# Layer 0's mixer of a two-layer decoder trunk: projections in seven block products, and the order of the output gate and the decays

## The chip, the cores and the metric

One core of a Trainium2 chip runs the whole program: two decoder layers on a sequence of 512 tokens of 1024 features. The metric is the device time of one execution in microseconds (us); the number given is a median over runs.

## The reference

Each layer is a half-step SwiGLU feed-forward, a mixer, and another half-step feed-forward. The change is inside the mixer of layer 0, the "hybrid" mixer (condensed):

```python
def hybrid_mixer(h, w_in, ...):                       # h: 512 x 1024, already normalised
    z, xbc, dt_raw, qm, km, vm, om, ig, fg = split_cols(h @ w_in, HY_SPLITS)
    xbc = jax.nn.silu(causal_dwconv(xbc, conv_w, conv_b))
    xs, bm, cm = split_cols(xbc, ...)                 # 1024, 256, 256 wide
    dt = jax.nn.softplus(dt_raw + dt_bias)
    y = ssd_chunked(xs, dt, A, bm, cm, 128) + xs * d_skip   # 16 heads, scan over chunks
    y = rms_norm(y * silu(z), ssd_norm)               # in 2 groups of 512 features
    hm = mlstm_chunked(qm, km, vm, ig + igate_bias, fg + fgate_bias, 128)   # 4 heads
    hm = rms_norm(hm, mlstm_norm) * sigmoid(om)       # per head of 256 features
    return concatenate([y, hm]) @ w_out               # 2048 -> 1024
```

The parts of `h @ w_in` are Z (1024 columns), xBC (1536), the gates (24), queries and keys (512 each), values (1024) and the output gate `om` (1024). All is float32. A float32 product is done on TensorE as three products of rounded parts: with x = xh + xl and w = wh + wl it takes xh·wh + xh·wl + xl·wh.

## The kernel before

**Engines and forms.** TensorE (PE) multiplies. A block of weights is loaded by SyncE (SP) into one of four `raw` buffers (128 x 1024 floats, 512 KB) and brought into a `form` buffer of high and low parts: `split` (L236 to L242) copies the high part on ScalarE (ACT, L239) and subtracts it on VectorE (DVE, L242). The feed-forward has a second way, a "summed" form: ACT writes the negated rounded copy into the low part's place (L529), GpSimd (POOL) issues a DMA that adds the raw block to it (L530), and ACT writes the high part (L531); DVE takes no part. `form` (L257) has the same way, but only for the mixer of layer 1. `mm3` (L277 to L282) issues the three matmuls of a product; PSUM collects the sum.

**Feed-forward: seven block products.** Both sides of a product are cut into 2x2 blocks, and seven products of sums and differences of blocks give the four blocks of the result, in place of eight (`seven`, L621). It needs seven block combinations of the activations (`xf`), four subtractions of weight blocks, and additions out of PSUM. The order on each engine is worked out by a planner (`Plan`).

**Mixer of layer 0.** Here the engines' order is the program's order, and generators are interleaved by `weave(main, filler, ratio)` (L53): after each step of `main`, `ratio` steps of `filler` are issued. Every engine works through its own list in that order, so an instruction that waits holds up what stands behind it on its engine. `hybrid` (L947) does, one after the other:

1. xBC by six pieces of 256 columns (`conv`), woven with the gates. All projections use `xgn`, the activations times the norm's gain as high and low parts; the row factor of the norm (`rrow`, or `rcol` for token-major output) is applied when PSUM is read.
2. `ssd`, the scan: 16 steps (4 chunks of 128 tokens, 4 quarters of 4 heads). A quarter's `decays` loads rows of cumulated decay by DMA, subtracts (DVE), masks (POOL `affine_select`), takes the exponential (ACT) and multiplies (DVE); `outputs` multiplies it with the values on TensorE. The decays are issued one quarter ahead of the outputs. Filler of the weave, at 1.35 to 1: queries, keys (`gemm_feat`, tile pqk), values, output gate (`gemm_tok`, tile ptok), in matmuls that stream 512 columns.
3. `mlstm`, 4 chunks; each multiplies its numerator (`pn`) into the output gate's tile `og`, and at the chunk's end scales it by the norm's factor. Then `og` is transposed (pht) into `hh`, `hl`. Filler, at 0.8 to 1: `gate`, that is Z (tile pz, 512 columns), SiLU, product with the scan's output and its norm by groups.
4. `project`: `[y, hm] @ w_out` (tile po), added to the residual, in weight pieces of rows 0 to 4, 8 to 16 and 4 to 8 (times 128).

Tiles come from pools by name and tag; a tile whose buffers are all taken waits for the release of the oldest. PSUM has 4 banks for tag mm, and pairs of banks (`ps_two`, tags pA and pB) that the feed-forward uses.

Of the kernel before, what the change touches and what calls it, by code (L numbers as in the profile page):

```python
# [44 lines left out]
NMIX = dict(mix0=10, mix1=15)  # L45
# [168 lines left out]
class Trunk:  # L214
# [21 lines left out]
    def split(self, hi, lo, src, eng="act"):  # L236
        nc = self.nc
        if eng == "act":
            nc.scalar.activation(hi, src, AF.Copy)  # L239
        else:  # L240
            nc.vector.tensor_copy(hi, src)
        nc.vector.tensor_tensor(lo, src, hi.bitcast(F32), op=ALU.subtract)  # L242
# [14 lines left out]
    def form(self, raw):  # L257
# [181 lines left out]

    def spread(self, cols, n, name):  # L440
# [10 lines left out]
    def rows_from(self, src, name):  # L451

        rows = self.tmp.tile([P, 4, P], F32, name=name, tag="rows", bufs=4)
        self.nc.sync.dma_start(rows, src.rearrange("n p -> (n p)").partition_broadcast(P).rearrange("q (n p) -> q n p", p=P))
        return rows
# [316 lines left out]
    def prep_later(self, which, k, last, squares=True, half=None):  # L772
# [5 lines left out]
        if k == 0 and not half:  # L778
            self.which = which
            self.xgn = [[Lazy(lambda: self.part.tile([P, 4, T], F32R, name="xgn", tag="xg")) for _ in range(2)] for _ in range(2)]  # L780
            squares4 = Lazy(lambda: self.tmp.tile([P, 4, T], F32, name="ssq", tag="ssq", bufs=1))
# [165 lines left out]
    def hybrid(self, nxt):  # L947
# [6 lines left out]
        weave(  # L954
            self.gates(w, ((0, DT0, 16), (16, F0, 4), (20, I0, 4)), g),
            chain(*(self.conv(w, X0, cp, xs, bc) for cp in (4, 5, 0, 1, 2, 3))),
            1.0,
        )

        q, k = self.slot("q"), self.slot("k")  # L960
        v = self.tmp.tile([P, 2, 2, 4, 257], F32, name="v", tag="v", bufs=1)
        v = [v[:, i] for i in range(2)]
        og = []

        def projections():
            for t, c0, sc in ((q, Q0, 128 ** -0.5), (k, K0, 1.0)):
                for cp in range(2):
                    W = self.wload(w[:, c0 + cp * 256 : c0 + cp * 256 + 256])
                    W = list(W)
                    for m in range(2):  # L970
                        ps = self.mmps("pqk")
                        self.gemm_feat(ps, W, m)
                        self.mark = nc.vector.scalar_tensor_tensor(
                            t[:, 2 * cp + m], ps, sc, self.rrow, op0=ALU.mult, op1=ALU.mult
                        )
                        yield
            for t in v:
                with self.tc.issue_after(self.mark.ins):
                    nc.vector.memset(t[:, :, :, 256:257], 1.0)
            for h in (0, 2):  # L980
                yield from self.gemm_tok(w, V0 + h * 256, 512, lambda b, ps, h=h: nc.scalar.activation(
                    v[b // 2][:, b % 2, h : h + 2, 0:256], ps.rearrange("p (h n) -> p h n", h=2), AF.Copy,
                    scale=self.rcol[:, b : b + 1]))
            og.extend(self.slot("og", F32, (2, 4, 256)) for _ in range(2))
            for h in (0, 2):
                yield from self.gemm_tok(w, O0 + h * 256, 512, lambda b, ps, h=h: nc.scalar.activation(
                    og[b // 2][:, b % 2, h : h + 2], ps.rearrange("p (h n) -> p h n", h=2), AF.Sigmoid,
                    scale=self.rcol[:, b : b + 1]))

        weave(self.ssd(xs, bc, g), projections(), 1.35)  # L990

        hid = [None] * 16

        def mlstm():
            yield from self.mlstm(q, k, v, og, g)
            hh, hl = self.feat("hh", KC, F32R), self.feat("hl", KC, F32R)
            for c in range(KC):
                pt = self.aux("pht", (T,))
                for b in range(NB):
                    nc.tensor.transpose(  # L1000
                        pt[:, b * P : (b + 1) * P], og[b // 2][:, b % 2, c // 2, (c % 2) * P : (c % 2 + 1) * P],
                        self.ident,
                    )
                self.split_gain(hh[c], hl[c], pt, self.par[:, 116 + c : 117 + c])
                hid[KC + c] = (hh[c], hl[c])
                if c % 2:
                    yield

        weave(mlstm(), self.gate(w, Z0, xs, hid), 0.8)
        self.project(a["hy_w_out"][0], hid, 1.0, nxt, ((0, 4), (8, 16), (4, 8)), 2)  # L1010

# [22 lines left out]
    def gate(self, w, Z0, xs, hid):  # L1034

        nc = self.nc
        for grp in range(2):
            for cp in range(2):
                c0 = Z0 + grp * 512 + cp * 256
                W = list(self.wload(w[:, c0 : c0 + 256]))  # L1040
                for m in range(2):
                    c = 4 * grp + 2 * cp + m
                    ps = self.mmps("pz")
                    self.gemm_feat(ps, W, m)
                    t1 = self.tmp.tile([P, T], F32, name="t1", tag="t1")
                    nc.vector.tensor_tensor(t1, ps, self.rrow, op=ALU.mult)
                    nc.scalar.activation(t1, t1, AF.Silu)
                    nc.vector.tensor_tensor(xs[c], xs[c], t1, op=ALU.mult)
                    if c % 4 == 0:
                        ssq = self.tmp.tile([P, T], F32, name="ssq", tag="ssq", bufs=1)  # L1050
                        nc.scalar.activation(ssq, xs[c], AF.Square)
                    else:
                        sq = self.tmp.tile([P, T], F32, name="sq", tag="t2")
                        nc.scalar.activation(sq, xs[c], AF.Square)
                        nc.vector.tensor_tensor(ssq, ssq, sq, op=ALU.add)
                    yield
# [3 lines left out]
            nc.scalar.activation(r, self.rows_of(rc).rearrange("p a b -> p (a b)"), AF.Copy)  # L1060
            yh, yl = self.slot("yh", F32R), self.slot("yl", F32R)
            for j in range(4):
                c = 4 * grp + j
                nc.vector.tensor_tensor(xs[c], xs[c], r, op=ALU.mult)
# [3 lines left out]
    def gemm_tok(self, w, c0, n, evac):  # L1068

        ps = [self.mmps("ptok", (512,)) for _ in range(NB)]  # L1070
        for k0 in range(0, KC, 2):
            W = self.form(self.raw(w[k0 * P : (k0 + 2) * P, c0 : c0 + n].rearrange("(k p) n -> p k n", p=P), 2, n))
            for b in range(NB):
                tok = slice(b * P, (b + 1) * P)
                for j in range(2):
                    k = k0 + j
                    self.mm3(
                        ps[b][:, 0:n],
# [815 lines left out]
```

## Time and profile before

| | |
|---|---|
| time, median of 3 runs | 2016.77 us (2015.88 to 2018.02) |
| the profiled execution's own time | 2019.29 us |
| its span, first to last instruction | 2017.6 us |
| mean granted TensorE clock | 0.992 |
| layer 0's mixer in it, about | 353 to 757 us |
| DVE forms of layer 0's mixer (L242, 128x1024) | 60 in the whole run, 1240 ns each |
| accumulating DMAs (form<-raw, POOL) | 136, of which none in this mixer |

A row of instruction groups reads: line, engine, operation, output<-input with shape, xcount | busy us, mean ns of one | idle time of the engine just before them, with what ended it. A row of windows reads: stretch, its length, busy us (count) of PE, PE's weight load, DVE, ACT, POOL, granted clock (1.00 is full), DMA share, GB/s. A row of the timeline reads: start, duration, engine, line, operation, tiles.

### The profile page before, as it was taken

What the parts mean: (1) busy time and instruction counts of PE and PEld (TensorE: products, weight loads), DVE (VectorE), ACT (ScalarE), POOL (GpSimd) and SP (SyncE); (2) the same over time, 40 slices, a digit from 0 to 9 for tenths busy, and PEclk for the clock granted to TensorE, in tenths of its full rate; (3) what the DMA queues carried; (4) which work ended last, traced back from release to release, by engine and by line L of the source; (5) the groups of instructions that cost most, each with busy time, mean ns of one, the idle gap of its engine ahead of it and who ended that gap; (6) DMA issues with size and microseconds to landing.
All of it is one profiled execution on the core that took longest, in us unless ns stands there. A gap on an engine that the chain in (4) does not pass through costs nothing.

```text
span 2017.6 us, 34412 instructions
## 1 busy us (share of the span) xinstructions
PE 1984.4 (98%) x13892; PEld 1800.6 (89%) x13892; DVE 1581.4 (78%) x2340; ACT 1170.2 (58%) x1716; POOL 270.1 (13%) x335
## 2 busy tenths in 40 slices
PE   8999999999999999999999999999999999999998
PEld 6999999787788888999998899999965678999998
DVE  6898878886547648988888898978679847988886
ACT  6666657442345434666565575756667644757565
POOL 1000101321101011010002010101215321101010
PEclk9999999999999999999999999999899999999999
DMA  7556566433331232666565356656754202656564
GB/s 210 136 148 167 150 164 148 125 107 115 103 96 63 82 97 63 168 157 162 155 152 149 94 148 167 161 153 160 191 116 105 53 16 69 157 158 165 150 168 115
DMA packets 214439, 265.49 MB, mean 132 GB/s; under 512 B 14140, under 2 KB 187400, under 8 KB 214280
## 3 DMA queue, kind: packets, MB, share of 16 engines
q1 hardware_dynamic: 193632, 190.87, 30.5%
q0 software_dynamic: 20448, 72.36, 19.2%
q8 instruction: 109, 1.79, 0.4%
q14 instruction: 50, 0.41, 0.1%
q10 hardware_dynamic: 200, 0.06, 0.0%
HBM read 188.77 MB, written 2.14 MB: 95 GB/s over the span
## 4 chain that ended last, share of the span: by engine, by line
PE 86%; DVE 5%; DMA 4%; issue 2%; ACT 1%; POOL 1%; SPq 0%; ACTq 0%; POOLq 0%; DVEq 0%
PE pA L281 9%; PE pA L280 9%; PE pA L282 9%; PE pD L280 5%; PE pD L281 5%; PE pD L282 5%; PE pB L280 2%; PE pB L281 2%; PE pB L282 2%; DMA form<-raw 2%; PE po L280 2%; PE po L282 2%; PE po L281 2%; PE ptok L280 2%; PE pu L282 2%
## 5 line engine op out<-in xcount | busy, mean ns | idle before, releaser
L502 DVE TENSOR_TENSOR form<-raw,form 128x1024 fp32r<-128x1024 f32 (+1 forms) x327 | 388.0, 1191 | 113.2 <-ACT form L500 112.3
L500 ACT ACTIVATE form<-raw 128x1024 fp32r<-128x1024 f32 (+1 forms) x327 | 334.6, 1027 | 177.3 <-DVE raw L495 120.6
L280 PE MATMUL pA<-xf,form 128*128 128x256 f32 x1152 | 322.1, 280 | 0.0
L281 PE MATMUL pA<-xf,form 128*128 128x256 f32 x1152 | 321.8, 279 | 0.0
L282 PE MATMUL pA<-xf,form 128*128 128x256 f32 x1152 | 321.4, 279 | 0.0
L495 DVE TENSOR_TENSOR raw<-raw 128x1024 f32<-128x1024 f32 (+2 forms) x241 | 283.6, 1180 | 17.4 <-DMA raw<-in_ffn_w_down 8.6
L530 POOL DMA_DIRECT2D form<-raw x136 | 116.9, 860 | 1202.7 <-ACT form L529 1142.4
L529 ACT ACTIVATE form<-raw 128x1024 fp32r<-128x1024 f32 (+1 forms) x136 | 140.1, 1031 | 140.3 <-PE pD L282 77.4
L280 PEld LDWEIGHTS pA<-xf,form 128*128 128x128 f32 x1152 | 216.4, 188 | 0.2
L282 PEld LDWEIGHTS pA<-xf,form 128*128 128x128 f32 x1152 | 216.1, 188 | 0.0
L281 PEld LDWEIGHTS pA<-xf,form 128*128 128x128 f32 x1152 | 215.8, 187 | 0.2
L281 PE MATMUL pA<-hid,form 128*128 128x256 f32 x704 | 198.6, 282 | 2.8 <-DVE hid L502 2.8
L280 PE MATMUL pA<-hid,form 128*128 128x256 f32 x704 | 198.8, 282 | 0.5 <-ACT hid L500 0.4
L282 PE MATMUL pA<-hid,form 128*128 128x256 f32 x704 | 197.4, 280 | 0.0
L280 PE MATMUL pD<-xf,form 128*128 128x256 f32 x576 | 161.2, 280 | 0.0
L281 PE MATMUL pD<-xf,form 128*128 128x256 f32 x576 | 161.2, 280 | 0.0
L282 PE MATMUL pD<-xf,form 128*128 128x256 f32 x576 | 161.0, 280 | 0.0
L495 DVE TENSOR_TENSOR ft<-ft 128x256 f32<-128x256 f32 (+2 forms) x288 | 146.1, 539 | 4.6 <-ACT ft L748 1.2
L531 ACT ACTIVATE form<-raw 128x1024 fp32r<-128x1024 f32 (+1 forms) x136 | 138.6, 1021 | 0.0
L281 PEld LDWEIGHTS pA<-hid,form 128*128 128x128 f32 x704 | 132.3, 188 | 4.7 <-DVE hid L502 4.6
L280 PEld LDWEIGHTS pA<-hid,form 128*128 128x128 f32 x704 | 132.6, 188 | 1.3 <-ACT hid L500 0.6
L282 PEld LDWEIGHTS pA<-hid,form 128*128 128x128 f32 x704 | 132.3, 188 | 0.0
(447 smaller groups left out, 5191.5 us busy)
## 6 DMA issues: line engine op xcount, KB each, us to landing
form<-raw POOLq DMA_DIRECT2D x120, 512.0 KB, 5.6
raw<-in_ffn_w_gate SPq DMA_DIRECT2D x88, 512.0 KB, 3.8
raw<-in_ffn_w_up SPq DMA_DIRECT2D x88, 512.0 KB, 4.0
raw<-in_ffn_w_down SPq DMA_DIRECT2D x64, 512.0 KB, 4.4
raw<-in_hy_w_in SPq DMA_DIRECT2D x44, 512.0 KB, 3.5
raw<-in_ffn_w_down SPq DMA_DIRECT2D x32, 384.0 KB, 3.4
raw<-in_hy_w_out SPq DMA_DIRECT2D x16, 512.0 KB, 3.3
form<-raw POOLq DMA_DIRECT2D x16, 384.0 KB, 4.2
```

What stands on the lines that cost most here:

```text
L280: mm(out, l[0], r[0], start=start, stop=False)
L281: mm(out, l[0], r[1], start=False, stop=False)
L282: mm(out, l[1], r[0], start=False, stop=stop)
L495: (self.p if pool else self.v)(n, lambda: e.tensor_tensor(out(), x(), y(), op=op), reads, writes)
L500: self.s(n, lambda: nc.scalar.activation(hi(), src(), AF.Copy), srck, hik)
L502: n, lambda: nc.vector.tensor_tensor(lo(), src(), hi().bitcast(F32), op=ALU.subtract), srck + hik, lok
L529: self.s(n, lambda: nc.scalar.activation(f()[:, 1], raw, AF.Copy, scale=-1.0), rawk, lok)
L530: self.plan.add("gpsimd", 0.85, lambda: nc.gpsimd.dma_start(f()[:, 1], raw, accum_op=ALU.add), rawk + lok, lok, 5.5)
L531: self.s(n, lambda: nc.scalar.activation(f()[:, 0], raw, AF.Copy), rawk, hik)
```

## The change

- Values (2 products of 512 columns), keys (1), Z (2) and the output gate (2) are done by a new `seven_now`, seven block products each, in the program's order (no planner). Each block is 24 matmuls that stream 256 columns into a pair of PSUM banks with tag pA, of which there are two. Queries, xBC and the gates keep their matmuls; the queries move ahead of the scan, into the weave with the new `xforms_now`, which makes the seven block combinations of the normalised activations (with the row factor in them).
- `form`'s summed way now belongs to layer 0's mixer where `summing` is set: four of seven forms in each `seven_now`, and all forms of xBC, queries and the output projection.
- `gemm_tok` goes. The output gate comes last, with nothing beside it, and each of its blocks is used at once: `x = v * r * o`, where `v` now holds the mLSTM's numerators (one more ACT copy per head and chunk) and `rs` the norm's factors.
- The scan's decays are two quarters ahead; `btok`, `cbs` are made per chunk. `mlstm` updates a head's state right behind its numerator.
- Several pools' tiles give way to one tile with fixed places (`room`); `NMIX` goes from 10 to 12; the ratios are 1.8 for the scan and 1.5 for the mLSTM; `project` takes its rows in the order 0 to 4, 4 to 8, 8 to 16.

```diff
     def form(self, raw):
...
-        if self.stage == "mix1":
+        if self.stage == "mix0" and self.summing:
             nc.scalar.activation(f[:, 1], raw, AF.Copy, scale=-1.0)
             nc.gpsimd.dma_start(f[:, 1], raw, accum_op=ALU.add)
             nc.scalar.activation(f[:, 0], raw, AF.Copy)
...
+        early = early()
+        weave(gates, early, 1.0)
+        weave(early, self.xforms_now(xf), 0.4)
...
+        def kept(dest):
+            def keep(i, ps):
+                act(dest(*((1, 0), (0, 1), (1, 1))[i]), ps, AF.Copy)
+            def done(a, j, ps):
+                if (a, j) == (1, 0):
+                    act(dest(1, 0), ps, AF.Copy)
+                else:
+                    tt(dest(a, j), ps, dest(*((1, 0) if a + j == 0 else (a, j))), op=ALU.add)
+            return keep, done
+        def values():
...
             for h in (0, 2):
-                yield from self.gemm_tok(w, V0 + h * 256, 512, lambda b, ps, h=h: nc.scalar.activation(
...
+                yield from self.seven_now(w, V0 + h * 256, xf, True, *kept(lambda a, j, h=h: v[a][:, :, h + j, 0:256]))
+            yield from self.seven_now(w, K0, xf, False, *kept(lambda a, j: k[:, 2 * j : 2 * j + 2, a * H : a * H + H]))
-        weave(self.ssd(xs, bc, g), projections(), 1.35)
+        weave(self.ssd(xs, bc, g), values(), 1.8)
...
+        def output_gate():
             for h in (0, 2):
+                def gated(a, j, o, h=h):
+                    for b in range(2):
+                        x = v[a][:, b, h + j, 0:256]
+                        nc.vector.scalar_tensor_tensor(
+                            x, x, rs[2 * a + b][:, h + j : h + j + 1], o[:, b], op0=ALU.mult, op1=ALU.mult
+                        )
+                yield from self.seven_now(w, O0 + h * 256, xf, True, *passing(gated, AF.Sigmoid))
+        mlstm = self.mlstm(q, k, v, rs, g)
+        zgate = self.gate(w, Z0, xs, hid, xf, passing)
+        weave(mlstm, zgate, 1.5)
+        drain(output_gate())
...
+    def xforms_now(self, xf):
...
+        for q in range(4):
+            t = self.big.tile([P, 8, H], F32, name="fx", tag="fx", bufs=1)
+            for m in range(2):
+                nc.vector.scalar_tensor_tensor(
+                    t[:, 2 * m : 2 * m + 2], self.xT[:, 2 * q + m].rearrange("p (a b) -> p a b", a=2),
+                    self.gain(self.which, 2 * q + m), row, op0=ALU.mult, op1=ALU.mult,
+                )
+            yield
+            tt(t[:, 4], t[:, 1], t[:, 3], op=ALU.add)
+            tt(t[:, 5], t[:, 4], t[:, 0], op=ALU.subtract)
+            tt(t[:, 6], t[:, 0], t[:, 1], op=ALU.subtract)
+            tt(t[:, 7], t[:, 2], t[:, 5], op=ALU.subtract)
+            for form, i in ((self.A11, 0), (self.A12, 2), (self.A22, 3), (self.S1, 4), (self.S2, 5), (self.S3, 6), (self.S4, 7)):
+                self.ready = self.split(tiles[form][:, 0, q], tiles[form][:, 1, q], t[:, i])
...
+    def seven_now(self, w, c0, xf, rows, keep, done):
...
+        pair = lambda: self.ps_two.tile([P, 2, T], F32, name="pw", tag="pA")
+        A = pair()
+        keep(0, mul(A, made(b11), self.A11, True))
+        yield
+        B = pair()
+        done(0, 0, mul(B, made(b21, True), self.A12, True))
+        yield
+        less(b11, b12, b11)
+        less(b12, b22, b12)
+        f22 = made(b22)
+        less(b22, b22, b11)
+        keep(1, mul(A, made(b22), self.S2, False))
+        yield
+        D = pair()
+        keep(2, mul(D, made(b11, True), self.S1, True))
+        yield
+        done(1, 1, mul(A, made(b12, True), self.S3, False))
+        yield
+        done(0, 1, mul(D, f22, self.S4, False))
+        yield
+        less(b21, b21, b22)
+        done(1, 0, mul(A, made(b21, True), self.A22, False))
+        yield
...
         block(0)
-        ahead = decays(0, 0)
+        ahead = [decays(0, 0)]
         for i, (c, q) in enumerate(steps):
-            now = ahead
-            if i + 1 < len(steps):
-                if q == 3:
-                    block(c + 1)
-                ahead = decays(*steps[i + 1])
+            while len(ahead) < 3 and i + len(ahead) < len(steps):
+                c1, q1 = steps[i + len(ahead)]
+                if not q1:
+                    block(c1)
+                ahead.append(decays(c1, q1))
             yield
-            outputs(c, q, *now)
+            outputs(c, q, *ahead.pop(0))
...
-    def mlstm(self, q, k, v, og, g):
+    def mlstm(self, q, k, v, rs, g):
...
-                tt(oc[:, h], oc[:, h], pn[:, 0:256], op=ALU.mult)
...
+                nc.scalar.activation(vc[:, h, 0:256], pn[:, 0:256], AF.Copy)
...
-            tt(oc, oc, r.unsqueeze(2).to_broadcast([P, 4, 256]), op=ALU.mult)
+            rs.append(r)
```

`mul` inside `seven_now` is the loop over two halves of 128 and four steps of K around `mm3`; `made` sets `summing` and calls `form`; `less` subtracts in place on DVE. `passing`, for Z and the output gate, keeps three blocks in rooms by ACT copies, adds the later block from PSUM on DVE, applies SiLU or sigmoid on ACT and hands the block on.

More of the change, by code (lines that the diff above doesn't have):

```diff
@@ L44 @@
 PERIODS = [(p, _pieces(p, 4)) for p in (2 * math.pi * 512, 2 * math.pi)]
-NMIX = dict(mix0=10, mix1=15)
+NMIX = dict(mix0=12, mix1=15)
 NRAW, NFORM = 4, 5
@@ L1272, in state @@
         def state(c):
+            pt = self.aux("pbt", (2, P))
+            for n in range(2):
+                nc.tensor.transpose(pt[:, n], bc[:, n, c * P : (c + 1) * P], self.ident)
+            nc.scalar.activation(btok, pt, AF.Copy)
             xe = xd[c]
             tt(xe, xe, g["de"][:, c].unsqueeze(2).to_broadcast([P, 16, 64]), op=ALU.mult)
-            new = st if c else self.tmp.tile([P, 16, 64], F32, name="st", tag="st", bufs=1)
+            new = st if c else self.room("st", 16, 64)
             if c:
```

247 lines of the change are left out of this document (127 added, 120 removed).

## The prediction

> **What bounds the kernel now.** I read the busy times first, then the chain of work that ended last, then the windows by stage, since one average over stages with different limits says little.
>
> ```profile
> span 2017.6 us, 34412 instructions
> ...
> PE 1984.4 (98%) x13892; PEld 1800.6 (89%) x13892; DVE 1581.4 (78%) x2340; ACT 1170.2 (58%) x1716; POOL 270.1 (13%) x335
> ...
> PE 86%; DVE 5%; DMA 4%; issue 2%; ACT 1%; POOL 1%; SPq 0%; ACTq 0%; POOLq 0%; DVEq 0%
> ```
>
> TensorE is busy for 98% of the span and is 86% of the chain. Layer 0's mixer runs from about 353 to 757 us. The windows of its stages (length, then busy time and instruction count of PE, weight load, DVE, ACT, POOL, then granted clock, DMA share and GB/s), and of two stretches of the feed-forward behind it, are:
>
> ```profile
> 353.00:431.30 78.30, 78.30 (x375) 63.11 (x374) 66.00 (x107) 33.36 (x44) 22.21 (x16) 1.00 0.35 110
> 431.30:596.00 164.70, 164.70 (x878) 128.69 (x877) 95.94 (x153) 65.62 (x89) 20.50 (x20) 1.00 0.36 112
> 596.00:664.70 68.70, 68.70 (x339) 58.03 (x338) 50.64 (x105) 33.10 (x82) 6.72 (x6) 1.00 0.16 54
> 664.70:757.00 92.30, 92.30 (x419) 75.83 (x418) 44.64 (x60) 34.05 (x45) 8.63 (x6) 1.00 0.31 98
> 353.00:757.00 404.00, 404.00 (x2004) 325.67 (x2003) 257.22 (x424) 166.12 (x257) 58.06 (x48) 1.00 0.31 99
> 836.00:870.00 34.00, 33.84 (x287) 33.64 (x286) 32.14 (x42) 22.22 (x28) 3.40 (x4) 1.00 0.54 136
> 757.00:840.00 83.00, 83.00 (x524) 74.80 (x523) 71.78 (x101) 47.74 (x66) 9.41 (x10) 1.00 0.41 108
> ```
>
> The first five are, in order, convolution; queries, keys, values and output gate beside the SSD scan; Z beside the mLSTM; and the output projection; and the mixer as a whole. In all of it TensorE is never idle at the full granted clock, so TensorE time taken out counts in full, unless another engine now makes it wait. DVE (257 of 404) and ACT (166) have room as an average; the question is whether they have it in each stage.
>
> **TensorE's own time.** A product of 512x1024 by 1024x512 is 96 matmuls of 512 columns in the old form (4 output tiles, 8 steps of K, 3 matmuls for the high and low parts), and 7 blocks of 24 matmuls of 256 columns (2 tiles, 4 steps, the same 3) in the new one. What one costs is its cadence, not its duration, since neighbours overlap. First and last of runs without a gap (start, duration): 26 matmuls, 24 matmuls and 49 matmuls.
>
> ```profile
> 438.99 0.40 PE L281 MATMUL pqk<-xgn,form 128*128 128x512 f32 x1
> 444.71 0.39 PE L282 MATMUL pqk<-xgn,form 128*128 128x512 f32 x1
> ...
> 589.93 0.40 PE L280 MATMUL ptok<-form,xgn 128*128 128x512 f32 x1
> 595.30 0.40 PE L282 MATMUL ptok<-form,xgn 128*128 128x512 f32 x1
> ...
> 203.32 0.28 PE L280 MATMUL pA<-xf,form 128*128 128x256 f32 x1
> 208.97 0.28 PE L280 MATMUL pD<-xf,form 128*128 128x256 f32 x1
> ```
>
> That is 5.72/25 = 0.2288 us, 5.37/23 = 0.2335 us, and 5.65/48 = 0.1177 us for the narrow ones of the feed-forward, which already works in seven block products. Values and output gate lose 384 matmuls (89.7 us), keys 96 and Z 192 (65.9 us): 155.6 us go. Seven products (values 2, keys 1, Z 2, output gate 2) of 168 narrow matmuls are 1176 x 0.1177 = 138.4 us. **TensorE gains 17.2 us.** The instruction order of the changed kernel as built has just these 1176, so the work does shrink. The two fewer transposes and the SSD's shift of state work are left at nothing: they are about a microsecond of a 404 us stage.
>
> **What DVE and ACT are given.** The prices:
>
> ```profile
> L242 DVE TENSOR_TENSOR form<-raw,form 128x1024 fp32r<-128x1024 f32 x60 | 74.3, 1240 | 48.5 <-ACT form L239 46.6 <-PE pxd L1225 1.5
> L495 DVE TENSOR_TENSOR raw<-raw 128x1024 f32<-128x1024 f32 x208 | 253.2, 1220 | 16.4 <-DMA raw<-in_ffn_w_down 7.7 <-DMA raw<-in_ffn_w_up 6.7
> L495 DVE TENSOR_TENSOR ft<-pA,ft 128x512 f32<-128x512 f32 x60 | 41.4, 691 | 35.9 <-PE pA L282 35.3
> L582 DVE SCALAR_TENSOR_TENSOR ft<-raw 128x512 f32<-128x512 f32 x32 | 22.2, 747 | 18.2 <-ACT raw L768 18.2
> L495 DVE TENSOR_TENSOR ft<-ft 128x256 f32<-128x256 f32 x176 | 67.8, 421 | 2.5
> L239 ACT ACTIVATE form<-raw 128x1024 fp32r<-128x1024 f32 x60 | 63.2, 1057 | 114.0 <-PE ptok L282 34.3 <-PE po L281 29.7 <-PE pxbc L281 15.4
> L646 ACT ACTIVATE ft<-pA 128x512 f32<-128x512 f32 x120 | 71.6, 596 | 102.7 <-PE pA L282 95.0 <-DVE hid L502 6.7
> ```
>
> One product costs DVE 4 subtractions of weight blocks (4 x 1.22), 3 low parts (3 x 1.24) and 3 additions out of PSUM (3 x 0.69): 10.7 us. On ACT it is 3 high parts and two copies for each of 4 "summed" forms, 11 x 1.057, and 3 copies out of PSUM of 0.596: 13.4 us, in 168 x 0.1177 = 19.8 us of TensorE. Either fits alone; what matters is what runs beside it.
>
> *Convolution and queries.* TensorE has 78.3 us, and 22.0 for the 96 query matmuls. DVE had 66.0; twelve convolution forms become summed (-14.9), four scalings of the queries come in (2.8) and the seven blocks of x are made here: 8 x 0.747, 16 x 0.421 and 28 low parts of 256 at about 0.42, 24.5 us. 78.4 us in 100.3: I take no cost. If the blocks come late, the first value product waits; their spread over the queries' matmuls speaks against it.
>
> *Values and keys beside the scan.* The forms' share of the old stage and of Z:
>
> ```profile
> 431.30:596.00 164.70, 140.06 (x577) 106.35 (x575) 29.51 (x24) 25.34 (x24) 0.00 (x0) 1.00 0.36 112
> 596.00:664.70 68.70, 51.91 (x193) 35.87 (x194) 9.78 (x8) 8.53 (x9) 0.00 (x0) 1.00 0.16 54
> ```
>
> TensorE: 164.7 - 192 x 0.2288 - 89.7 + 504 x 0.1177 = 90.4 us. DVE: 95.94, less 29.51 of forms and 8 scalings of queries and keys (5.5), is 60.9, plus three products (32.0): 92.9. Neighbouring instructions overlap a little:
>
> ```profile
> 862.33 2.35 DVE L502 TENSOR_TENSOR form<-raw,form 128x1024 fp32r<-128x1024 f32 x2
> ```
>
> Two took 2.35 us instead of 2.48; some 0.09 over 30 added instructions takes off 3 us, to 90. So **DVE has as much to do as TensorE in this stage**. The most that the trace shows DVE sustain beside a full TensorE is 32.14 of 34 us, 94.5%, in an order written by a planner (836 to 870); from 757 to 840 it is 86%. 90/0.945 = 95.2 gives 4.9 us of idle TensorE, 90/0.86 gives 14. The bounds are 0 (the neighbouring stages take some work over) and 15; I take 5, by the row in which DVE is the tight engine. The decays made two steps ahead serve this: with one step, each quarter's chain (row load, subtraction, select, exponential, product) must fit in half the old time.
>
> *Z beside the mLSTM.*
>
> ```profile
> L1356 ACT ACTIVATE hsq<-pn 128x256 f32<-128x256 f32 x16 | 6.0, 377 | 0.0
> ...
> L1047 ACT ACT_TABLE_LOAD x2 | 2.6, 1283 | 0.2 <-DVE t L1046 0.2
> L1336 ACT ACT_TABLE_LOAD x1 | 1.3, 1283 | 0.0
> ```
>
> TensorE: 68.7 - 43.9 + 336 x 0.1177 = 64.3. ACT: 33.1 - 8.5 of forms + 22 x 1.057 + 6 x 0.596 + 16 copies of the mLSTM's numerators at 0.377 + table loads. The built order has seven in place of three here, so 4 x 1.283: 62.6 us, 97%. Overlap of ACT's neighbours lowers that by up to a tenth. By the same reckoning as for DVE, 0 to 10 us; I take 4. DVE has 50.6 - 9.8 + 2 x 10.7, less 8 scalings of Z (0.69), 16 products with the output gate (0.42) and 4 of 1024 (1.22) that go or move out, 45 us: not tight.
>
> *Output gate, alone.* 39.5 us of TensorE (DVE: 21.3 and 16 x 0.48, 29 us) with nothing beside it but its own forms. The chain that could be late is that of the raw buffers and the accumulating DMA:
>
> ```profile
> L530 POOL DMA_DIRECT2D form<-raw x136 | 116.9, 860 | 1202.7 <-ACT form L529 1142.4
> ...
> form<-raw POOLq DMA_DIRECT2D x120, 512.0 KB, 5.6
> ...
> raw<-in_hy_w_in SPq DMA_DIRECT2D x44, 512.0 KB, 3.5
> ```
>
> Second block's matmuls done (2 x 2.82 us), then copy 1.06, issue 0.86, accumulation 5.6, next raw load 3.5 into the freed buffer, and copy, issue and accumulation again: 24.2 us, where the next product wants it after 19.8 + 2.8 = 22.6. That is 1.6 us; I take 2 for both (0 to 4). The 16 gated products of 0.48 us lie beside matmuls, except the last.
>
> *Output projection.* Its 16 forms become summed: DVE 44.6 - 19.8, ACT 34.1 + 17, both far below 92. Nothing. The 60 more accumulating DMAs are 52 us of issue on POOL, spread over 390 us.
>
> **The sum.** 17.2 us less work, 11 us of new idle (5 + 4 + 2): 6.2 us. The profiled execution took 2019.29, 1.7 over its span and 2.5 over the median, and would become 2013.1; against the median, 2016.77 - 6.2 = **2010.6 us**. Without new idle it would be 1999.6. About 0.2%, 4 us, is what measurement can tell from no change.
>
> **The rivals.**
>
> *All covered* (under 3 us of idle): 1999.6 to 2002.5. For it: DVE and ACT have slack on either side of both tight stages. Against: two engines at 90 to 100%. Chance 0.09.
>
> *DVE sets the pace of values, keys and scan* at the 86% or below of the stretch at 757: 14 to 20 us idle there in place of 5, and the gain is gone: about 2019. Chance 0.15, no measurable change.
>
> *PSUM is freed too late.* A block is 24 x 0.1177 = 2.82 us, and only two pairs of banks serve the products, so TensorE may start a block only when the block before last has been read. The reading instruction (0.6 to 0.69) stands in its engine's order behind whatever was put there: two subtractions of 1.22 ahead of it make 3.13, 0.3 too late, three 1.5 too late; a table load and two copies on ACT (1.28 + 2.1 + 0.6) 1.2 too late. There are 49 blocks; at 17.2/49 = 0.35 us a block on average the gain is gone, and at 0.53, a delay of 1.1 us at every other block, it is 26 us: **2026, slower**. For it: the order is woven by fixed ratios, with scan work between. Against: the feed-forward does the same with PE at 99.5%. Chance 0.20.
>
> *The clock.*
>
> ```profile
> PE gm L281 <- DVE iw L502: 3.4, 1, 3.4
> ...
> 1670.00:1680.00 10.00, 9.13 (x54) 8.45 (x53) 5.16 (x9) 4.44 (x8) 4.42 (x3) 0.76 0.21 65
> 1680.00:1690.00 10.00, 10.00 (x43) 8.12 (x42) 3.42 (x6) 2.13 (x4) 0.00 (x0) 0.90 0.01 2
> ```
>
> Around a norm at 1670, where TensorE waited for 0.87 us amid small work, the granted clock fell to 0.76 and 0.90 over 20 us: 3.4 us lost beyond the wait. Six such spells in the thin stages lose 20 us and their waits, some 5 more: 1999.6 + 25 + part of the 11 = about 2031. The mixer shows 1.00 throughout, so 0.04. The Trainium skill, "TensorE: Matmul & The Clock Gate", section "What's actually happening", has the clock halved only after an idle window of about 3.4 us; by that, waits of a microsecond as in the rival before would cost no clock, and this rival falls away.
>
> *Table switches cost double.* If ACT stood still behind each load as long as the load takes, the four more in Z (1.28 each) would add 5.1 us to a stage in which ACT has nothing to spare: 2015.7, no measurable change. The rows of the loads speak against it (0.2 us of idle before all three), so 0.03. The Trainium skill, "ScalarE: Activation LUTs", section "What ACT_TABLE_LOAD costs", speaks for it: a switch is a load of 1283 ns, which the rows agree with, and a drain of some 1380 ns, which they do not show; by my estimate from that page it would be 5.5 us.
>
> That it does not do what it says is excluded by the built order.
>
> **Chances.** The forecast of 2010.6 (its own range 2003 to 2016) has 0.49; all covered 0.09; DVE's pace 0.15; PSUM 0.20; clock 0.04; table switches 0.03. Faster by over 0.2% (the first two): 0.58; within (DVE's pace, switches): 0.18; slower: 0.24. The range from 2000 to 2026 holds the forecast, DVE's pace, most of "all covered" and the lower half of PSUM.
>
> **What would show it.** Right: narrow matmuls of the new products at 0.118 us; mixer end near 750; TensorE idle of about 5 us between values and keys with DVE over 90%, and ends of wait on DVE's weight and PSUM instructions; ACT over 90% in Z. Wrong: idle of TensorE over 15 us, above all ended by the readers of PSUM pairs or by a landing accumulation; granted clock below 1.00 in the mixer; or DVE's busy sum over the mixer far from 267 us (78 + 90 + 45 + 29 + 25 by stage).

## The result: slower, against the forecast

The changed kernel takes 2046.12 us (median of 4 runs, 2044.69 to 2048.55), the kernel before 2017.31 beside it: a ratio of 1.0145, 95% interval 1.0127 to 1.0163, or 29 us more. 2010.6 was forecast, with 2026 as the upper end.

The page of the changed kernel, first its busy times, then the chain that ended last:

```profile
span 2042.9 us, 35775 instructions
...
PE 1975.9 (97%) x14394; PEld 1820.8 (89%) x14394; DVE 1587.0 (78%) x2393; ACT 1264.1 (62%) x1857; POOL 324.3 (16%) x395
...
PE 81%; DMA 7%; DVE 6%; ACT 3%; issue 2%; POOL 1%; SPq 0%; ACTq 0%; POOLq 0%; DVEq 0%
```

On the chain TensorE went from 86% to 81%, and DMA from 4% to 7%. The mixer of the kernel before, from the same point to its last matmul of the output projection, is

```profile
357.00:757.50 400.50, 400.50 (x1978) 322.88 (x1978) 253.72 (x421) 164.50 (x255) 56.16 (x47) 1.00 0.31 98
```

The changed kernel's windows by stage (they end at the last matmul of queries, scan, mLSTM, output gate and output projection; the last row is all of them) are:

```profile
357.00:456.20 99.20, 97.83 (x440) 77.76 (x439) 73.22 (x151) 57.86 (x88) 39.80 (x30) 1.00 0.75 173
456.20:580.60 124.40, 107.25 (x895) 96.75 (x893) 89.53 (x149) 68.61 (x97) 29.87 (x32) 0.96 0.69 168
580.60:641.00 60.40, 58.82 (x407) 56.20 (x406) 44.00 (x84) 50.36 (x114) 10.71 (x12) 0.95 0.42 99
641.00:704.60 63.60, 51.32 (x372) 48.50 (x371) 31.19 (x59) 38.05 (x52) 11.65 (x13) 0.92 0.73 166
704.60:787.50 82.90, 82.90 (x371) 68.68 (x369) 21.51 (x33) 39.65 (x48) 17.73 (x18) 1.00 0.81 193
357.00:787.50 430.50, 398.11 (x2475) 347.89 (x2474) 259.45 (x474) 254.53 (x393) 109.76 (x105) 0.97 0.69 164
```

The mixer is 30.0 us longer. Idle time of TensorE (length less busy): 1.4, 17.2, 1.6, 12.3 and 0, in all 32.4 us, where there was none. No engine is full in the two bad stages: DVE has 89.5 of 124.4 us beside the scan and 31.2 of 63.6 in the output gate. DMA's share has gone from 0.31 to 0.69. And the granted clock, 1.00 before, is 0.92 to 0.96 in three stages, 0.97 over the mixer. Busy time should have gone to 400.5 - 17.2 = 383.3; it is 398.1, or 14.8 more. So 30.0 = 32.4 + 14.8 - 17.2. Not all of the 14.8 us is the clock: the granted clock was 0.50 in four stretches of 3.4 us and two of 6.8, from 494.4, 545.6, 576.3, 624.1, 661.6 and 688.9 us on. Their sum, with the busy time of TensorE in them, is

```profile
sum 27.29, PE 21.44; mean PE 3.57
```

At full clock the work in them would have taken half, so the clock cost 10.7 us. The other 4.1 us are open. My estimate is that most of them stand at the ends of runs of matmuls: there are 18 gaps of TensorE, and the last matmul before a gap counts with its whole duration (0.28 us) where the others count with the distance to the next (0.12 us), some 3 us in all.

Behind the mixer the profiles differ by 4.7 us the other way (1260.1 and 1255.4 us): there the stretches at 0.50 add up to 30.5 us before and 21.5 after. One stretch of the feed-forward shows it, before and after:

```profile
1057.50:1157.50 100.00, 97.95 (x616) 87.98 (x615) 85.46 (x111) 57.74 (x83) 13.96 (x11) 0.97 0.43 118
```

```profile
1087.50:1187.50 100.00, 98.07 (x635) 88.00 (x634) 87.39 (x116) 58.32 (x85) 13.99 (x11) 1.00 0.45 123
```

The waits of TensorE in the mixer, longest groups (us in all, times, longest):

```profile
PE pw L280 <- ACT rooms L1030: 6.8, 4, 5.1
PE py L1362 <- DVE rooms L1349: 5.0, 1, 5.0
PE pw L280 <- DVE rooms L1038: 4.0, 2, 3.2
PE pw L280 <- ACT k L1001: 3.4, 1, 3.4
PE psl L1384 <- DVE rooms L1378: 2.9, 1, 2.9
```

Three of five are a new block (pw) that waits for the reader of its PSUM pair on ACT or DVE. That looks like the rival "PSUM is freed too late". But in the longest wait of each of these three groups the reader had itself just been held up: L1001 (3.4 us) stood behind a wait of ACT of 8.04 us for a row, L1038 (3.2) and L1030 (5.1) behind waits of ACT of 6.67 and 4.76 us for raw weight blocks. The engines were not idle all the while, though: of the 17.2 us in which TensorE stood still beside the scan, ACT computed during 10.6 and DVE during 11.7, and through the fifth row's 2.9 us DVE computed without a pause, ACT for 2.84 us. The waits of DVE in the scan's stage, and of SP's queue in the whole mixer, the last row from the kernel before:

```profile
DVE rooms L1343 <- ACT rooms L1341: 15.7, 4, 7.8
DVE rooms L1343 <- DMA rooms<-arows: 8.2, 3, 5.1
```

```profile
SPq L254 <- DMA form<-raw: 260.9, 49, 28.3
SPq L470 <- PE py L1364: 22.5, 6, 12.1
```

```profile
SPq L254 <- DVE form L242: 262.8, 47, 12.0
```

L1341 and L1343 are the first users of a quarter's row of decays (L1341 on ACT must have read it before DVE overwrites it). L254 loads a raw weight block: it waits for the accumulating DMA that still reads the buffer, and L470, the row load, stands behind it on SP. The sum of these waits proves nothing by itself, since the loads of the kernel before waited just as long in all, for DVE's forms; only the longest is new (28.3 us, 12.0 before). New too is that the row loads wait at the head of the queue for a place: in the scan's stage 52.1 us in all for the instructions that still use it (by the profile PE's `py` and `pbt` and DVE's L1349), where the kernel before has 0.4 us of waits for `py`. That kernel has four buffers for rows and works one quarter ahead, the changed one three places and two quarters ahead.

The longest wait of the scan's stage (573.7 to 578.7 us) shows the row loads in it; first SP's queue, then ACT, then DVE (start, duration):

```profile
568.49 0.38 SPq L254 DMA_DIRECT2D raw<-in_hy_w_in  x1
568.96 0.50 SPq L470 DMA_DIRECT2D rooms<-mrows  x1
```

```profile
574.35 1.28 ACT L1348 ACT_TABLE_LOAD   x1
575.64 0.63 ACT L1348 ACTIVATE rooms<-rooms 128x512 f32<-128x512 f32 x1
```

```profile
577.25 0.69 DVE L1425 TENSOR_TENSOR rooms<-raw,rooms 128x512 f32<-128x512 f32 x1 [2.19 <-DMA rooms<-mrows]
577.86 0.69 DVE L1349 TENSOR_TENSOR rooms<-rooms 128x512 f32<-128x512 f32 x1
```

The row of the mLSTM is asked for half a microsecond after the raw load got its buffer, lands 8.27 us later, and only then DVE gets on to L1349, which makes the decays that TensorE's `py` waits for. L1349 itself needed nothing of that row: its own input was ready at 576.27, so the row cost it 1.6 of the 5.0 us. The rest came before. The quarter's own row landed at 571.74, 6.45 us after a load that had waited 12.1 us for its place, and ACT's exponential (L1348), whose input was there at 574.21, began 1.4 us later, behind a load of its function table.

The landing times in the mixer (queue, count, KB, median us from issue to landing), before and after:

```profile
raw<-in_hy_w_in SPq DMA_DIRECT2D x40, 512.0 KB, 3.5
raw<-in_hy_w_out SPq DMA_DIRECT2D x16, 512.0 KB, 3.3
arow<-arows SPq DMA_DIRECT2D x16, 256.0 KB, 3.8
```

```profile
form<-raw POOLq DMA_DIRECT2D x60, 512.0 KB, 5.6
raw<-in_hy_w_in SPq DMA_DIRECT2D x40, 512.0 KB, 4.9
raw<-in_hy_w_out SPq DMA_DIRECT2D x16, 512.0 KB, 5.3
rooms<-arows SPq DMA_DIRECT2D x16, 256.0 KB, 6.3
```

The accumulations take the 5.6 us that the feed-forward showed; what I had not counted is that each plain load beside them becomes 1.4 to 2.5 us slower. In the output gate the chain of waits holds (start, duration in us):

```profile
648.95 8.34 DMA raw<-in_hy_w_in
...
676.12 7.25 DMA form<-raw
...
683.41 6.03 DMA raw<-in_hy_w_out
```

The clock is seen in the matmuls of the output gate, behind a wait of 5.1 us:

```profile
692.06 0.58 PE L280 MATMUL pw<-form,xf 128*128 128x256 f32 x1 [5.10 <-ACT rooms L1030]
692.44 0.41 PE L281 MATMUL pw<-form,xf 128*128 128x256 f32 x1
692.66 0.41 PE L282 MATMUL pw<-form,xf 128*128 128x256 f32 x1
...
695.93 0.28 PE L280 MATMUL pw<-form,xf 128*128 128x256 f32 x1
696.05 0.28 PE L281 MATMUL pw<-form,xf 128*128 128x256 f32 x1
```

Behind the first they start some 0.21 us apart, from 695.8 on 0.12 us. So this long wait is paid again in the 3.7 us behind it, by some 1.7 us.

### The profile page after: what moved, and what is told of

Read it like the earlier page. It is cut to its first block, busy times and chain, and to the rows that moved or that the text cites. A ratio compares the mean times of both kernels' runs of the same rounds, so it can differ in the third digit from the quotient of the medians.

```text
span 2042.9 us, 35775 instructions
## 1 busy us (share of the span) xinstructions
PE 1975.9 (97%) x14394; PEld 1820.8 (89%) x14394; DVE 1587.0 (78%) x2393; ACT 1264.1 (62%) x1857; POOL 324.3 (16%) x395
## 4 chain that ended last, share of the span: by engine, by line
PE 81%; DMA 7%; DVE 6%; ACT 3%; issue 2%; POOL 1%; SPq 0%; ACTq 0%; POOLq 0%; DVEq 0%
PE pA L281 10%; PE pA L280 10%; PE pA L282 10%; PE pD L280 5%; PE pD L282 5%; PE pD L281 5%; DMA form<-raw 3%; PE pB L280 3%; PE pB L282 3%; PE pB L281 3%; PE po L280 2%; PE po L282 2%; PE po L281 2%; DMA rooms<-arows 1%; PE pu L280 1%
## 5 line engine op out<-in xcount | busy, mean ns | idle before, releaser
L280 PEld LDWEIGHTS pA<-xf,form 128*128 128x128 f32 x1152 | 218.9, 190 | 0.4 <-DVE ft L511 0.2
L281 PEld LDWEIGHTS pA<-xf,form 128*128 128x128 f32 x1152 | 218.9, 190 | 0.2
L282 PEld LDWEIGHTS pA<-xf,form 128*128 128x128 f32 x1152 | 218.8, 190 | 0.0
L281 PEld LDWEIGHTS pA<-hid,form 128*128 128x128 f32 x704 | 132.9, 189 | 4.6 <-DVE hid L518 4.6
L662 ACT ACTIVATE ft<-pA 128x512 f32<-128x512 f32 x120 | 71.5, 595 | 103.1 <-PE pA L282 95.3
L280 PEld LDWEIGHTS pA<-hid,form 128*128 128x128 f32 x704 | 133.0, 189 | 1.4 <-ACT hid L516 0.6
```

The source lines that it names most:

```text
L280: mm(out, l[0], r[0], start=start, stop=False)
L281: mm(out, l[0], r[1], start=False, stop=False)
L282: mm(out, l[1], r[0], start=False, stop=stop)
L662: self.s(T, lambda: nc.scalar.activation(to(), ps()[:, :, 0:H], AF.Copy), [(*psk, 0), (*psk, 1)], tok)
```

## Experiments

Theories at the start. **A:** accumulating DMAs hold raw buffers and SP's queue, so rows and weights come late. **B:** DVE's own work sets the pace. **C:** PSUM pairs are read late because of what ACT and DVE compute. Each run was timed against the kernel before on its own chip (medians 2020.5 to 2023.0 there); the ratios to it, with 95% intervals, are to be held against the changed kernel's 1.0145. A thousandth is 2 us. All edits are to the changed kernel unless said otherwise.

**e1_no_sum**

```diff
-        if self.stage == "mix0" and self.summing:
+        if False:
```

> All forms of the mixer are made by ACT and DVE again; no accumulating DMA in it. Theory A (the accumulating DMA keeps a raw buffer taken until it lands, the next raw loads wait for it at the head of SP's queue, and the decay rows behind them come late): the wait of raw loads for form<-raw goes from SP's queue, TensorE's idle time between scan start and Z falls from 17 to under 8 us and in the output gate from 12 to under 5; DVE gets 60 x 1.24 = 74 us more, which costs in the convolution, where it is already full: 2030 to 2038 us in all. Rival B (DVE's own work sets the pace of the scan): 2065 to 2080 us, with DVE over 95% there. Rival C (pairs of PSUM banks read too late because of what the engines compute): idle stays near 32 us, 2046 to 2060.

1.0076 (1.0055 to 1.0097), 14 us less than the changed kernel. Output gate and Z, with no accumulation, have 5.9 and 0 us of idle. But the scan's stage keeps 20.7, now with DVE at 106.1 of 126.4 us:

```profile
459.80:586.20 126.40, 105.71 (x853) 94.89 (x854) 106.14 (x173) 56.80 (x86) 23.25 (x17) 0.91 0.35 99
```

On the base of 2017.31 that is 2032.6, in A's range, yet A's forecast for the scan fails: a loss is there without a single accumulation, and with rows that land in 3.5 us. It need not be the same loss, for DVE has 16.6 us more to do. B's 95% of DVE does not come (84%), but DVE computes during 19.0 of the 20.7 us in which TensorE stands still. This run alone does not decide between late rows and DVE's work; e9 and e11 do more.

**e2_rows_on_act**

```diff
-        self.nc.sync.dma_start(rows, ...)
+        self.nc.scalar.dma_start(rows, ...)
```

> The rows of decays (and of the mLSTM) are loaded from ACT's queue, so that they no longer stand behind raw loads in SP's. Theory A: the waits of DVE and ACT for these rows (some 35 us in all) shrink by half or more and TensorE's idle in scan and values falls by 6 to 10 us: 2034 to 2041 us. Rivals B and C: within 3 us of 2046. If it is DMA bandwidth that makes rows late and not the queue, issue to landing stays 6 us and the time stays at 2046.

1.0103 (1.0080 to 1.0126): 8 us less, with intervals that all but touch. The time is in A's range, but rows land in 4.3 us instead of 6.3, and idle in the scan goes only from 17.2 to 13.8. Standing behind raw loads in SP's queue is a part of the rows' lateness, no more.

**e3_gate_split**

```diff
-        if self.stage == "mix0" and self.summing:
+        if self.stage == "mix0" and self.summing and not self.late:
...
+        self.late = True
         drain(output_gate())
```

> Only the forms of the output gate and the output projection are split by ACT and DVE again. Theory A: the 12 us of idle in the output gate fall below 4 and its granted clock goes from 0.91 to 0.97 or more: 2030 to 2037 us. Rival C: the waits for ACT's and DVE's reads of the PSUM pairs remain (10 us there), 2044 to 2048. Rival B says nothing of this stage, where DVE is 44% busy.

1.0081 (1.0059 to 1.0103): 13 us less. The output gate's window, whose start and contents are the same:

```profile
641.00:694.60 53.60, 49.10 (x372) 47.31 (x372) 44.90 (x71) 30.62 (x43) 2.96 (x3) 0.97 0.40 118
```

63.6 us become 53.6: idle 12.3 to 4.5, clock 0.92 to 0.97, DVE 31.2 to 44.9 us and no harm from it. This is A, and the waits of new blocks for the PSUM readers on ACT and DVE, which C would keep, fall from 9.7 to 3.1 us.

**e4_one_ahead**

```diff
-            while len(ahead) < 3 and i + len(ahead) < len(steps):
+            while len(ahead) < 2 and i + len(ahead) < len(steps):
```

> Decays one step ahead as in the kernel before, all else as changed. Theory A: rows are asked for one step later while they stand behind the same raw loads, so the scan waits longer: 2046 to 2058 us. Rival D (two steps ahead puts waiting instructions in front of DVE's and ACT's other work): 2036 to 2043 us.

1.0155 (1.0132 to 1.0178): not to be told from the changed kernel, so D falls, and A, whose range begins there, is neither helped nor hurt. The second step ahead neither saves nor costs anything that can be measured.

**e5_gates_first** and **e6_ratio_135.** A further theory, E: the gates' 25 small DVE steps end at 451 us instead of 423, because the blocks of x stand between them, and TensorE's filler is used up before the scan begins.

```diff
+                with self.tc.issue_after(self.gated.ins):      # e5: the copy that spreads the decays
                     nc.vector.scalar_tensor_tensor(t[:, 2 * m : 2 * m + 2], ...)
...
-        weave(self.ssd(xs, bc, g), values(), 1.8)
+        weave(self.ssd(xs, bc, g), values(), 1.35)             # e6
```

> One order is added: DVE starts the seven blocks of x only after the gates' last step (the copy that spreads the cumulated decays). Theory E (the blocks of x stand between the gates' 25 small dependent DVE steps, so the decays are known at 457 us, the scan's first output comes at 478, and the value products, TensorE's filler, are used up before the scan is): the decays are spread by about 430, the first output comes by 460, idle of TensorE from the end of the queries to the scan's last output falls from 17 to under 9 us: 2034 to 2042 us where the changed kernel has 2046. Theory A (raw loads and accumulating DMAs make the rows late): the scan starts earlier, but its idle time stays at 14 us or more: 2044 to 2050.

> The scan's ratio is 1.35 again, so that the 21 blocks of values and keys last for all 16 steps. Theory E: less TensorE work ahead of the scan and more at its end; idle in that stage falls by 3 to 8 us: 2038 to 2043. Theory A: no change, 2046 within 3 us. If the order on the engines does not follow the ratio, no change either.

e5: 1.0143 (1.0126 to 1.0159); e6: 1.0128 (1.0101 to 1.0154). Neither has the gain that E forecast: in e6 the scan's idle is 17.0 us, as it was. But e5 did not bring about the early start of the scan that it was meant to try. In it the decays are spread at 415.8 us, 41 us earlier, but the rows are still loaded only from 463 us on, and the scan's first output comes at 472 (478 in the changed kernel). The row loads start right behind the queries in both kernels, at 459 and 463; what binds them there (their buffers are parts of one large tile that is first written at 456.9, behind the queries) was not tried apart.

**e7_gates_gate_split** and **e8_gates_split_ratio_act** put these edits together: e3 and e5; and e2, e3, e5 and e6.

> The order of e5 together with split forms in the output gate and the output projection. If the two causes are apart, the gains add: 11 us from the forms and what the gates' order alone gives, 2022 to 2032 us where the changed kernel has 2046.

> As the run before, with rows loaded from ACT's queue and the scan's ratio at 1.35. If all four add: 2014 to 2026 us, at or below the kernel before; if rows and ratio act on the same idle time as the gates' order, no more than 3 us from the run before.

1.0090 (1.0059 to 1.0121) and 1.0137 (1.0105 to 1.0169). Of e7, whose forecast of 2022 to 2032 is missed (2035.5 on the base of 2017.31), all is e3's gain. e8 misses: in Z idle grows to 11.5 us. The rows on ACT's queue are not enough to explain it, for e2 has them there too, and 1.9 us of idle in Z. Of the 11.5 us, 8.7 lie behind two PSUM reads on ACT (L1031) that stood behind waits of 7.31 and 3.81 us for raw weight blocks; which of the four edits brought that about was not tried.

**e9_rows_by_pe**, for theory F: DVE and ACT work in order, and the first user of a late row holds up everything behind it. The row loads go; TensorE spreads the columns instead.

```diff
-            rows = self.rows_from(g["arows"][c, hs], "rows")
+            rows, e = self.rows_of(g["acs"][:, c, hs]), self.room("rows", 4, P)
...
-            rows = self.rows_from(g["mrows"][c], "mrows")
+            rows, e = self.rows_of(g["mt"][:, c]), self.room("mrows", 4, P)
```

> The rows of decays (16) and of the mLSTM (4) are no longer loaded by DMA: TensorE spreads the columns into PSUM by four transposes each (80 transposes, some 9 us of TensorE more), and DVE and ACT read them there. Theory F (DVE and ACT take their instructions in order; the one that reads a row waits 6 us and more for its DMA, and the reads of PSUM that TensorE needs stand behind it): idle in scan, values and keys falls from 17 to under 7 us and the clock there rises; 2040 to 2047 us in all with the 9 us of transposes. If it is the scan's own chain of dependent steps, and not the rows' arrival, idle stays over 12 us: 2050 to 2058.

1.0098 (1.0078 to 1.0118), 9 us less although TensorE does 80 transposes more. The scan's stage, and all its waits of TensorE that the profile finds:

```profile
456.60:564.80 108.20, 104.44 (x909) 95.12 (x907) 83.92 (x142) 65.49 (x92) 27.45 (x31) 0.99 0.63 144
```

```profile
PE py L1357 <- DVE rooms L1344: 3.7, 2, 2.9
```

124.4 us become 108.2, idle 17.2 becomes 3.8 and the clock 0.99, with the accumulations as they were. All waits of pw for L1001, L1005 and L1007, the PSUM readers, are gone, though those read what they did before: F, not C. Waits of raw loads for accumulations at the head of SP's queue are even longer than in the changed kernel (336.2 us in the mixer, 260.9 there), so these alone do not hold up the scan. The edit takes away more than the rows' landing, however: raw loads no longer stand behind row loads, no load waits for a row's place, and DVE no longer overwrites what ACT must read first. The last is small: at the wait of 3.4 us ACT began on its row at 542.35, and DVE could go on at 543.01. The first is worth about 3.4 us of idle (e2). Whether a fourth place for rows would have done what e9 does was not tried.

**e10_rows_by_pe_split** (e9 and e3) and **e11_rows_by_pe_no_sum** (e9 and e1).

> As the run before, with split forms in the output gate and output projection: the gains add up, 2028 to 2036 us. Otherwise 2040 to 2048.

> Rows by TensorE and no accumulating DMA at all. Theory B (DVE's own work sets the pace once the rows are there): the scan's stage stays at 120 us or more with DVE at 88% or more, 2036 to 2045 us. Theory F without B: that stage falls below 115 us, 2022 to 2032 us.

1.0051 (1.0031 to 1.0072): the two causes are mostly apart, 9 and 13 us become 19. e11: 1.0070 (1.0047 to 1.0094), 2031 on the base of 2017, and a scan's stage of 114.7 us: within what F without B gave, at the edge of both. DVE is at 101.8 us there, and the stage is 7 us longer than in e10. So once the rows are there, DVE's work does begin to set the pace in this stage, and summing the values' and keys' forms helps it; the times of e10 and e11 have overlapping intervals.

Four kernels, by one profile each, now settle what e1 left open. TensorE's idle time in the scan's stage is 17.2 us with row loads and sums, 20.7 with row loads and no sums (e1), 3.8 without row loads (e9) and 10.2 without either (e11). Taking the row loads away saves 13.4 us with accumulations beside them and 10.5 us without.

**e12_before_summed**, one part of the change alone, in the kernel before:

```diff
-        if self.stage == "mix1":
+        if self.stage == "mix0":
```

> The kernel before with one part of the change alone: all its 60 weight forms in this mixer are summed (ACT copies and an accumulating DMA). TensorE has no gap there, and 165 us for 16 steps of the scan. If accumulating DMAs alone are enough to hold it up: 4 us or more above the kernel before. If they only hurt where a stage is short: within 3 us of it.

1.0052 (1.0029 to 1.0074), 10 us slower than its own base: the first of the two readings. TensorE, which had no gap in this mixer, has 6.8 us of them in its profile, all before the scan: 1.5 and 0.7 at the convolution's first forms and 4.6 where the gates' last steps wait. Summed forms on their own cost time even where the stages are long.

**e13_rows_pe_late_split** and **e14_late_split_only.** Sums only in convolution (behind its first piece), queries, values and keys; rows by TensorE in e13, by DMA in e14.

```diff
             for cp in (4, 5, 0, 1, 2, 3):
+                self.summing = cp != 4
...
+        self.late = True
         mlstm = self.mlstm(q, k, v, rs, g)
```

> Rows by TensorE; summed forms only in the convolution behind its first piece, the queries, values and keys; split forms in Z, output gate and output projection. Theory: what is left of the loss are the gaps at the convolution's first form (1.4 us and the clock behind it), in Z and at the output gate's first form, where raw blocks wait for accumulations and ACT makes two copies a form: 4 to 8 us less than with sums in Z (ratio 1.001 to 1.003 to the kernel before). If the rest is the price of the transposes and of DVE's own work: ratio 1.004 to 1.006, as there.

> The same forms with the rows loaded by DMA on SP's queue as in the changed kernel. Theory F: the scan keeps its 15 us and more of idle: 6 to 12 us slower than the run before, though 9 us of transposes are gone. If the waits for rows came from the sums in Z and behind only: as fast as the run before or faster.

1.0048 (1.0030 to 1.0065) and 1.0064 (1.0047 to 1.0081). e13 misses its 1.001 to 1.003 and lies in the range of its rival, by which the rest is the price of the transposes and of DVE's work. In it the idle of convolution and Z is gone (0 us), but the median is that of e10: a single wait of 5.0 us at the scan's end and the clock behind it came in their place. e14 keeps 18.2 us of idle in the scan, so the rows' lateness does not come from the later sums; in the median it is 3 us behind e13, less than the 6 expected, with overlapping intervals. No version ran faster than the kernel before. What is left in e13 is 10 us of idle in its profile, a clock of 0.98 and the transposes (forecast at 9 us); which of these could still go is open.

## Why the prediction was wrong

**The work was sized right.** Narrow matmuls of the new products start 0.12 us apart at full clock, as forecast. DVE's sums by stage are 73, 90, 44, 31 and 22 us where 78, 90, 45, 29 and 25 were forecast, 259 against 267.

**"Values and keys beside the scan": 5 us taken, 17.2 measured, and above the bound of 15.** This is the step that failed first. I asked whether DVE has more work than TensorE and took the utilisation of another stage as its limit. DVE was 72% busy. What mostly limits is a latency: rows come by DMA, the order of ACT and DVE is fixed, and the first user of a late row keeps back the PSUM reads and the products behind it. From the scan's first output to its last, the 16 steps took 122 us before (7.6 each), 102 here (6.4), and 92 in e9 (5.7), which takes the rows' DMA away: 13 of the 17 us go. How much of the lateness is the landing and how much the wait for a place is open.

**"Output gate": 2 us taken, 12.3 measured.** The chain was named rightly: copy, accumulation, raw load, copy again. I priced it with landing times of the kernel before: 5.6 us, the median of the feed-forward's accumulations, which is also the median here, and 3.5 for raw loads at a DMA share of 0.31. In this stage, at 0.73, two raw loads on the chain took 8.34 and 6.03 us and one accumulation 7.25. e3 shows that the sums are the cause. My upper bound of 4 came from rows of a less loaded stretch.

**"Output projection: nothing" and the 52 us of issue on POOL.** TensorE has no gap there, so its own cost was nothing. But its first raw loads are on the output gate's path, since they share the four buffers; e3 took both sums away at once, so their parts are not apart.

**"Z": 4 us taken, 1.6 measured;** ACT was 50.4 of 60.4 us busy, not 62.6.

**The rival "DVE sets the pace" (0.15)** had the size right, 14 to 20 us of idle beside the scan, but by luck: DVE was 72% busy, not 86%, and in e9 the idle fell to 3.8 us with 83.9 us of DVE's work in place of 89.5.

**The rival "PSUM is freed too late" (0.20)** had the place and nearly the idle time (26 us, and 32.4 came), though not the time (2026), but the wrong reason: it counted instructions ahead of the reader, and what stood ahead in the longest of these waits was a wait.

**The rival "table switches cost double" (0.03)** does not show: in the longest wait of the scan the load took 1.28 us and the next instruction began 0.01 us behind it. Two such loads, of 1.28 us each, stood on ACT ahead of L1348 there all the same.

**The rival "the clock" (0.04)** was counted out because the mixer showed 1.00; but that was the state without gaps. With gaps, 10.7 us of the 17.2 us that TensorE gained went into it, where the sum had nothing. I had let the rival fall away for short waits by the rule of an idle window of about 3.4 us. The Trainium skill, "TensorE: Matmul & The Clock Gate", section "What's actually happening", which states that rule, fits the spells at the waits of 3.4, 5.0 and 5.1 us above by their length, though the clock fell already 2.6 and 2.0 us into the last two. It does not fit the waits of 2.9 and 3.2 us, which had a spell too, nor the next rows, where waits of 1.00 and 0.58 us, with eight matmuls of one column between, were followed by 3.4 us of matmuls about 0.21 us apart:

```profile
621.93 1.05 PE L416 MATMUL pssq<-raw,ssq 128*128 128x1 f32 x8 [1.00 <-ACT rooms L1471]
...
623.79 0.39 PE L280 MATMUL pw<-xf,form 128*128 128x256 f32 x1 [0.58 <-ACT rooms L1030]
...
624.40 0.42 PE L280 MATMUL pw<-xf,form 128*128 128x256 f32 x1
624.62 0.42 PE L281 MATMUL pw<-xf,form 128*128 128x256 f32 x1
```

So the sum failed in three terms: rows (12.2 us short), raw blocks (10.3) and the clock with what the gaps add to TensorE's busy time (14.8, of which the clock is 10.7); with 1.4 at the convolution's start and 2.4 that Z did not need, 36.3 us in the mixer. By the medians the forecast missed by 35.5.

## What to carry to other kernels

When TensorE's work in a stage shrinks, ask of every load that the stage needs whether it can start early enough and land in the new time of a step, not only whether each engine's busy time fits. Price a DMA by a row from a stretch with the DMA share that the stage will have. An accumulating DMA spares DVE, but it keeps its source buffer for 5.6 us in the median, 7.25 in the output gate, and slows the loads beside it; in the scan's stage, with the rows there, it spared 7 us (e10 against e11, by their profiles), and in the output gate, where raw buffers were short, it cost 10 (e3).

## What was not expected of the hardware

A plain load of 512 KB, 3.3 to 3.5 us at a DMA share of 0.31, took 4.9 to 5.3 at 0.69, and a spread row of 256 KB 6.3 instead of 3.8, the largest rise for the smaller transfer. And each of the five waits of TensorE of 2.9 to 5.1 us in this mixer went with a spell at half clock of 3.4 or 6.8 us, while single waits of up to 1.9 us had none. Two waits of 1.6 us in all with tiny matmuls between them had one.
